# The last down-projection of a decoder step cut into five token spans instead of four, the last two of 128 tokens

## The chip, the cores and the metric

One core of one Trainium2 chip runs the whole step. The metric is the time of one execution in device microseconds (us); the median of three runs of the kernel before is 2002.76 us (2002.69 to 2004.21).

## What is computed

One step of a decoder layer for 1056 tokens: 1024 tokens of a new sequence and 32 tokens of 8 running ones (4 each), all with 1024 features. A SwiGLU feed-forward half, a mixer (recurrence and short convolution), a second SwiGLU half, and a last RMSNorm. Each sub-layer is modulated by a conditioning vector (shift, scale, gate). What matters here is the end of it:

```python
    hn = modulate(rmsnorm(x, g_ffn2), mod[:, 6], mod[:, 7])
    x = x + 0.5 * mod[:, 8][:, None, :] * swiglu(hn, w2_gate, w2_up, w2_down)
    ...
    y_prompt = rmsnorm(xp, final_gain)
    y_sample = rmsnorm(xs, final_gain)
```

## The kernel before, in words

Activations lie transposed: features on the 128 partitions, in 8 blocks of 128 features (KD = 8), tokens along the free dimension (N = 1056, of which T = 1024 are the prompt). A float32 product is made of three float32r matmuls: each operand is split into a high and a low part, and `accumulate` (L416) issues high x high, high x low and low x high for each block of the contraction, one bank of PSUM collecting all of them. Each of these matmuls loads its own 128x128 weights; the moving operand is as wide as the token span.

Most of the work before the end uses a Strassen form. The down-projection of the second half ends in two plain pieces of 512 contraction rows: `back` (L698) does the first with all three 352-token spans beside each other, and `last2` (L1423) does the second through `back_by_span` (L707), which is the end stage. Its outer loop runs over the spans of `END_SPANS` (L38), its inner one over the 8 output blocks o. For each (span, o):

- TensorE: 12 matmuls (4 blocks of contraction by 3 parts) into one bank (`accumulate`, L420). All 8 blocks' weights stay in SBUF, split into high and low, from the first span on.
- VectorE: `add_back` (L685) adds the gated bank onto x (L687); in the span that holds the 32 sample tokens two small operations more (L691, L693).
- ScalarE: the square of the new x (`square_add`, L546), and x times the final gain (L720). VectorE adds the squares into two accumulators (L550), and joins them at o = 6 (L552).

When a span is done, a generator (`norm_then`, L728, and `stats`, L556) is queued. It is advanced once per o of the next span (from o = 1). Per span it cuts the tokens into pieces of at most 128: a 256-token span has 2, a 272-token span 3 (128, 128 and 16), a 128-token span 1. It then
- sums the squares over the partitions with matmuls against ones ("nrm", L566): 4 TensorE instructions a piece, as two accumulators times two instructions of a float32 matmul;
- turns them into 1/rms with five small VectorE operations (L569, L571 to L574) and one ScalarE square root (L570);
- scales an identity by it ("dg", L580), one VectorE operation a piece;
- after a lag (2 steps for the first span, 3 for the others) spreads it over the partitions with matmuls ("rb", L587), 2 TensorE instructions a piece.
Then `final` (L1416) multiplies x by it on VectorE in three steps (4, 2 and 2 feature blocks, L1419) and sends each to HBM on SyncE's queue (L1420). In the last span no matmuls are left to hide this: `flush` (L410, called at L1427) runs it to the end.

The order in which the engines take these instructions is the framework's scheduling of the traced program; in this stage no order is written out by hand.

Of the kernel before, what the change touches and what calls it, by code (L numbers as in the profile page):

```python
# [34 lines left out]

FIRST_SPANS = ((0, 352), (352, 176), (HALF, 352), (HALF + 352, 176))
QUARTERS = ((0, Q), (HALF, Q), (Q, Q), (HALF + Q, Q))
END_SPANS = ((800, 256), (0, 272), (272, 272), (544, 256))  # L38

COL = {}  # L40
NPAR = 0
# [197 lines left out]
def decoder_step(ctx, tc, xin, par, ada0, ada1, ada2, wada, wf, wga, wdn, wdl, wmi, wgt, wmo,  # L239
# [467 lines left out]
    def back_by_span(kind, idx, buf, ms, after, spans=SPANS, gain=None):  # L707

        ids = [u for i in idx for u in ws.take(kind, i)]
        left = len(adas[1])  # L710
        for c, sp in enumerate(spans):
            accs = []
            for o in range(KD):
                b = bank(f"bk{o}_{sp[0]}")
                ahead = min(AHEAD, 7 - o) if c == 0 else 3 if sp == spans[-1] and o > 3 else 0
                accumulate([b], [sp], ws.unit(ids[o], ahead), rows(ms), True, True)
                add_back(buf, o, sp, b)
                square_add(accs, sp, o, join=gain is not None)
                if gain is not None:
                    act.activation(x[:, o, of(sp)], x[:, o, of(sp)], AF.Identity, scale=col(gain, o, o + 1))  # L720
                if o > 0:
                    advance()
                if sp == spans[-1] or left > KD and c > 0:
                    more_ada(-(-left // (KD * (1 + (left > KD)))))
            sums.append((("n", sp), norm_then(accs, sp, after, int(c > 0), 2 if c == 0 else 3)))
        assert not adas[1]
# [696 lines left out]
    def last2(kind, buf, ms):  # L1423
        back_by_span(kind, [(1, h) for h in range(4)], buf, ms, final, END_SPANS, "gf")

# [124 lines left out]
```

## Time and profile before

| | us |
|---|---|
| median of 3 runs | 2002.76 |
| the profiled execution | 2002.88 |
| its span in the trace | 2000.8 |
| TensorE busy | 1945.4 (97% of the span) |
| VectorE busy | 1288.1 (64%) |
| ScalarE busy | 757.8 (38%) |

The span is the time from the first to the last instruction in the trace; the profiled execution's own time is 2.1 us longer, which lies around it. "PE" is TensorE's matmuls, "PEld" its weight loads, "DVE" VectorE, "ACT" ScalarE, "SPq" the queue on which SyncE issues transfers. A line number such as L420 is the kernel's.

### The profile page before, as it was taken

The page shows a single profiled execution, that of the slowest core. Times are in us where ns is not written, and L with a number is a line of the kernel's source. Part 1 is how long each engine was busy: PE and PEld are TensorE (multiplying, and loading weights), DVE is VectorE, ACT ScalarE, POOL GpSimd, SP SyncE. Part 2 cuts the span into 40 slices and gives each one's busy share as a digit, 9 for nine tenths or more (in the row PEclk, how much of TensorE's full clock was granted, in tenths as well). Part 3 has the DMA queues.
Part 4 walks back from the last instruction along what each step waited for, and adds up shares of the span by engine and source line. Part 5 has one row for each costly group of instructions (what it writes and reads, how often), then busy time and mean ns, then how long its engine had stood idle before and what let it go on. Part 6 is the DMA issues. An engine that isn't in the chain of part 4 may idle for free.

```text
span 2000.8 us, 36465 instructions
## 1 busy us (share of the span) xinstructions
PE 1945.4 (97%) x15188; PEld 1913.1 (96%) x15188; DVE 1288.1 (64%) x2519; ACT 757.8 (38%) x1330; POOL 126.1 (6%) x223
## 2 busy tenths in 40 slices
PE   3899999999999999999999999999999999999997
PEld 3789999999999999999999999999999999999997
DVE  5564555565467875584887768666555645878656
ACT  3442233333342432344443447433333333433324
POOL 0000000100011000000000010001000000100000
PEclk9899999999999999999999999999999999999999
DMA  7245455531254532011111122532322222742302
GB/s 253 77 165 190 165 175 185 190 117 65 86 192 144 194 113 91 22 48 53 48 43 54 43 79 76 178 132 101 120 81 102 92 86 98 258 148 90 140 33 87
DMA packets 89764, 230.67 MB, mean 115 GB/s; under 512 B 7776, under 2 KB 41568, under 8 KB 89600
## 3 DMA queue, kind: packets, MB, share of 16 engines
q1 hardware_dynamic: 64592, 137.40, 20.5%
q0 software_dynamic: 25008, 90.96, 12.7%
q8 instruction: 119, 1.95, 0.4%
q14 instruction: 45, 0.37, 0.1%
HBM read 180.63 MB, written 47.69 MB: 114 GB/s over the span
## 4 chain that ended last, share of the span: by engine, by line
PE 95%; DVE 3%; DMA 1%; ACT 1%; issue 0%; SPq 0%; DVEq 0%; ACTq 0%
PE bk L420 14%; PE up_a L459 13%; PE ga_a L459 13%; PE dn_a L459 9%; PE up_c L459 6%; PE ga_c L459 6%; PE dn_c L459 5%; PE up_b L459 3%; PE ga_b L459 3%; PE v L420 2%; PE dn_b L459 2%; PE b L420 2%; PE c L420 2%; PE x L420 2%; PE n L420 2%; PE ada L503 2%
## 5 line engine op out<-in xcount | busy, mean ns | idle before, releaser
L220 DVE TENSOR_TENSOR hl<-raw,hl 128x512 fp32r<-128x512 f32 x286 | 194.9, 687 | 202.7 <-ACT hl L219 202.3
L219 ACT ACTIVATE hl<-raw 128x512 fp32r<-128x512 f32 x286 | 175.8, 626 | 249.8 <-PE bk L420 104.6
L219 ACT ACTIVATE hl<-S_ga 128x512 fp32r<-128x512 f32 x176 | 111.0, 631 | 279.4 <-DVE S_ga L172 59.3
L459 PE MATMUL dn_a<-f,hl 128*128 128x264 f32 x1536 | 192.0, 284 | 0.1
L420 PE MATMUL bk<-ml,hl 128*128 128x352 f32 (+2 forms) x1248 | 189.5, 312 | 1.4 <-DVE x L687 1.4
L459 PEld LDWEIGHTS dn_a<-f,hl 128*128 128x128 f32 x1536 | 189.3, 188 | 0.3 <-ACT f L820 0.3
L420 PEld LDWEIGHTS bk<-ml,hl 128*128 128x128 f32 x1248 | 186.6, 188 | 1.9 <-DVE x L687 1.9
L220 DVE TENSOR_TENSOR hl<-S_ga,hl 128x512 fp32r<-128x512 f32 x176 | 121.4, 690 | 76.2 <-ACT hl L219 75.3
L687 DVE SCALAR_TENSOR_TENSOR x<-bk,modT,x 128x352 f32<-128x352 f32 (+6 forms) x160 | 81.4, 534 | 101.1 <-PE bk L420 100.4
L459 PE MATMUL ga_a<-hnT,hl 128*128 128x264 f32 x792 | 103.2, 286 | 0.0
L459 PE MATMUL up_a<-hnT,hl 128*128 128x264 f32 x792 | 102.7, 285 | 0.0
L459 PE MATMUL up_a<-hmT,hl 128*128 128x264 f32 x792 | 102.1, 284 | 0.0
L459 PE MATMUL ga_a<-hmT,hl 128*128 128x264 f32 x792 | 102.1, 284 | 0.0
L459 PEld LDWEIGHTS ga_a<-hnT,hl 128*128 128x128 f32 x792 | 98.9, 188 | 3.3 <-issue 0.8
L459 PEld LDWEIGHTS up_a<-hnT,hl 128*128 128x128 f32 x792 | 98.8, 188 | 2.5 <-ACT u1st L473 0.4
L459 PEld LDWEIGHTS up_a<-hmT,hl 128*128 128x128 f32 x792 | 98.8, 188 | 0.4 <-ACT u1st L473 0.4
L459 PEld LDWEIGHTS ga_a<-hmT,hl 128*128 128x128 f32 x792 | 98.8, 188 | 0.4 <-ACT g1st L473 0.4
L459 PE MATMUL dn_c<-f,hl 128*128 128x264 f32 x768 | 96.4, 284 | 0.0
L459 PEld LDWEIGHTS dn_c<-f,hl 128*128 128x128 f32 x768 | 94.8, 188 | 0.0
L821 DVE TENSOR_TENSOR f<-f 128x1056 fp32r<-128x1056 f32 x56 | 67.9, 1254 | 25.1 <-ACT f L820 25.1
L219 ACT ACTIVATE hl<-S_dn 128x512 fp32r<-128x512 f32 x64 | 39.9, 628 | 114.3 <-PE dn_a L459 29.7
L820 ACT ACTIVATE f<-f 128x1056 fp32r<-128x1056 f32 x56 | 57.7, 1078 | 48.2 <-DMA f<-mf 48.0
(455 smaller groups left out, 3722.1 us busy)
## 6 DMA issues: line engine op xcount, KB each, us to landing
raw<-wga SPq DMA_DIRECT2D x88, 512.0 KB, 3.4
f<-mf POOLq DMA_DIRECT2D x28, 1056.0 KB, 6.6
raw<-wada SPq DMA_DIRECT2D x56, 512.0 KB, 5.2
raw<-wdn SPq DMA_DIRECT2D x32, 512.0 KB, 3.4
mf<-mt POOLq DMA_DIRECT2D x48, 264.0 KB, 3.3
raw<-wmi SPq DMA_DIRECT2D x20, 512.0 KB, 3.2
ml<-ml POOLq DMA_DIRECT2D x16, 528.0 KB, 4.7
raw<-wdl SPq DMA_DIRECT2D x16, 512.0 KB, 3.3
```

Source lines behind the costliest of these rows:

```text
L219: self.nc.scalar.activation(hl[:, 0], src, AF.Copy)
L220: self.nc.vector.tensor_sub(hl[:, 1], src, hl[:, 0].bitcast(F32))
L420: pe.matmul(b[:, :sp[1]], hl[:, wh, k], rhs(k, h, sp), start=first and k == ks[0] and i == 0, stop=last and k == ks[-1] and i == 2)
L459: pe.matmul(b[:, 512 - Q + q * Q:512 + q * Q], hl[:, wh, k], forms[X_FORMS[i]][:, k, h, q * Q:q * Q + Q], start=new and k == 0 and j == 0, ...
L503: pe.matmul(ada_bank[u][32 * q:32 * q + 32, :ADA_W[u]], cst[:, k], raw[:, q], start=k == 0, stop=k == KD - 1, skip_group_check=True)
L687: dve.scalar_tensor_tensor(x[:, o, lo:lo + n], b[:, :n], modT[:, buf, GATE, o, 0:1], x[:, o, lo:lo + n], op0=ALU.mult, op1=ALU.add)
L820: act.activation(form[:, k:k + 2, 0], raw[:, k:k + 2], AF.Copy)
L821: dve.tensor_sub(form[:, k:k + 2, 1], raw[:, k:k + 2], form[:, k:k + 2, 0].bitcast(F32))
```

## The change

One line. The sample tokens (1024 to 1055) stay in the span that is done first, which now starts at 784 and is 272 tokens wide; then come 256, 272, 128 and 128 tokens. The 1056 tokens, the functions and the loops are the same; the outer loop of the end stage has five turns instead of four.

```diff
-END_SPANS = ((800, 256), (0, 272), (272, 272), (544, 256))
+END_SPANS = ((784, 272), (0, 256), (256, 272), (528, 128), (656, 128))
```

## Rows read from the trace of the kernel before

**Rows 1.** The page, part 1: busy time, share of the span, instructions of each engine.

```profile
PE 1945.4 (97%) x15188; PEld 1913.1 (96%) x15188; DVE 1288.1 (64%) x2519; ACT 757.8 (38%) x1330; POOL 126.1 (6%) x223
```

**Rows 2.** TensorE's timeline of the end: start, us, instructions in count, idle time before.

```profile
1950.24 0.95 PE L566 MATMUL nrm<-ones,sq 128*128 128x1 f32 x8
1951.05 3.24 PE L420 MATMUL bk<-ml,hl 128*128 128x272 f32 x24
1955.17 0.68 PE L587 MATMUL rb<-dg,ones 128*128 128x128 f32 x4 [0.88 <-DVE dg L580]
1955.61 10.80 PE L420 MATMUL bk<-ml,hl 128*128 128x272 f32 x84
1966.24 1.39 PE L566 MATMUL nrm<-ones,sq 128*128 128x1 f32 x12
1967.50 4.74 PE L420 MATMUL bk<-ml,hl 128*128 128x272 f32 x36
1972.08 0.74 PE L587 MATMUL rb<-dg,ones 128*128 128x128 f32 x6
1972.66 7.48 PE L420 MATMUL bk<-ml,hl 128*128 128x272 f32 x60
...
1986.15 3.07 PE L420 MATMUL bk<-ml,hl 128*128 128x256 f32 x24
```

**Rows 3.** The chain that ended last, after the last down-projection matmul: start, us, what.

```profile
1990.13 1.07 PE nrm L566 x8
...
1992.87 1.06 PE rb L587 x4
...
1993.96 1.22 DVE x L1419
...
1995.78 0.60 DVE x L1419
```

**Rows 4.** TensorE's timeline in two stretches, each of one width only.

```profile
1899.85 36.01 PE L420 MATMUL bk<-ml,hl 128*128 128x352 f32 x222
...
1935.98 11.38 PE L420 MATMUL bk<-ml,hl 128*128 128x256 f32 x95
```

**Rows 5.** 89.9 to 115.7 us, 352 and 176 wide by turns: weight loads, busy us, mean ns.

```profile
L942 PEld LDWEIGHTS second<-hn,hl 128*128 128x128 f32 x191 | 26.0, 189 | 0.0
```

**Rows 6.** Weight loads of the norm sums in the last span: start, us, count.

```profile
1979.86 1.43 PEld L566 LDWEIGHTS nrm<-ones,sq 128*128 128x128 f32 x12
```

**Rows 7.** Groups by line and shape, 1890 us to the end: busy us, mean ns.

```profile
L546 ACT ACTIVATE sq<-x 128x272 f32<-128x272 f32 x16 | 6.9, 430 | 10.4 <-DVE x L687 10.4
...
L546 ACT ACTIVATE sq<-x 128x256 f32<-128x256 f32 x16 | 6.7, 417 | 10.5 <-DVE x L693 5.5 <-DVE x L687 5.1
...
L687 DVE SCALAR_TENSOR_TENSOR x<-bk,modT,x 128x256 f32<-128x256 f32 x8 | 3.9, 481 | 2.6 <-PE bk L420 2.6
L687 DVE SCALAR_TENSOR_TENSOR x<-bk,modT,x 128x224 f32<-128x224 f32 x8 | 3.6, 451 | 2.2 <-PE bk L420 2.0
...
L1419 DVE TENSOR_TENSOR x<-x,rb 128x512 f32<-128x512 f32 x4 | 2.6, 680 | 0.0
...
L1419 DVE TENSOR_TENSOR x<-x,rb 128x1024 f32<-128x1024 f32 x2 | 2.4, 1222 | 1.0 <-PE rb L587 1.0
```

**Rows 8.** SyncE's queue at the end, and sizes of the output transfers with us to landing.

```profile
1995.24 1.96 SPq L1420 DMA_DIRECT2D yout<-x  x3
...
yout<-x SPq DMA_DIRECT2D x2, 512.0 KB, 3.0
yout<-x SPq DMA_DIRECT2D x4, 256.0 KB, 3.4
```

**Rows 9.** TensorE's timeline around 95 us, single matmuls: 352 and 176 wide by turns.

```profile
95.27 0.43 PE L942 MATMUL second<-hn,hl 128*128 128x176 f32 x2
...
95.35 0.35 PE L942 MATMUL second<-hn,hl 128*128 128x352 f32 x1
...
95.54 0.43 PE L942 MATMUL second<-hn,hl 128*128 128x176 f32 x2
```

## The prediction

> **What bounds the kernel now.** I read the busy times first, then TensorE's timeline over the last 50 us, then the chain that ended last. TensorE is busy for 97% of the span [rows 1]. In the end stage it goes from one group of matmuls to the next almost without a hole: one wait of 0.88 us, at 1955.17, for the first span's "dg" [rows 2]. So what is added to TensorE's stream here lengthens the kernel, and what VectorE and ScalarE do beside it costs nothing while they keep up. The last down-projection matmul ends at 1986.15 + 3.07 = 1989.22 [rows 2]. From there to the end of the span (2000.8) are 11.6 us in which one step waits for the other: squares, "nrm", 1/rms, "dg", "rb", the scaling by VectorE, and the output transfer [rows 3]. The change trades these two: more in the stream, less in the tail.
>
> **Term 1, the matmuls.** Each (span, block) takes 12 matmuls whatever its width, so a span is 96 of them, and four spans become five: 384 become 480. By width, two spans of 272 and one of 256 stay (their order changes, and all move together in one direction); one of 256 goes, two of 128 come. The price of one by width is the distance from start to start, not its duration in the trace, since matmuls overlap:
> - 352 columns: the stretch lasts 36.01 us and its last matmul hangs some 0.17 over the next start, as 1955.61 + 10.80 against 1966.24 shows [rows 2]; (36.01 - 0.17)/222 = 161 ns [rows 4].
> - 272 columns: (1966.24 - 1955.61)/84 = 126.5 ns [rows 2].
> - 256 columns: (11.38 - 0.17)/95 = 118 ns [rows 4].
>
> No row shows a stream of 128-column float32r matmuls. Two things lie near. In the kernel's first pair 352 and 176 columns alternate, each with its own 128x128 weights: (26.0 - 0.19)/190 = 136 ns a matmul, 272 a pair [rows 5]; less the 161 of the wide one, 110 are left for 176 columns. A straight line through 352 and 256 columns would give 118 - 80 x 0.45 = 82. So below some width a matmul stops getting cheaper. And the matmuls of "nrm", whose moving operand is one column, still load 128x128 weights at (1.43 - 0.19)/11 = 113 ns each [rows 6]. I read both as the same floor: a new set of weights every 110 ns or so, whatever streams through. 128 columns lie between one and 176, so I take 110 ns. The bounds: not above 118 (256 columns), and not below the 80 ns treated as a rival.
> Price: 192 x 0.110 - 96 x 0.118 = 21.1 - 11.3 = **+9.8 us** (at 118 ns +11.3).
>
> **Term 2, the norm's matmuls in the stream.** A 272-token span has three pieces, a 256-token span two, a 128-token span one. In both kernels that makes 10 pieces, but before 2 + 3 + 3 = 8 lie in the stream and 2 in the tail; after 3 + 2 + 3 + 1 = 9 and 1. A "nrm" block of 8 instructions takes 1951.05 - 1950.24 = 0.81 us, one of 12 takes 1.26; so one of 4 should take 0.36. The blocks in the stream go from 0.81 + 1.26 + 1.26 to 1.26 + 0.81 + 1.26 + 0.36: +0.36. "rb" blocks of 4 and 6 take 0.44 and 0.58 [rows 2], one of 2 about 0.22: by the same count +0.23. Each block costs a little where the wide matmuls resume: 36 of them after a block take 4.74 - 0.17 = 4.57 us, against 36 x 0.1265 = 4.55 [rows 2]. I round the sum to **+0.7 us**.
>
> **Term 3, the one wait in the stream.** The first span's norm has the shortest cover, 24 matmuls of the second span. They now are of 256 columns and not 272: 24 x (126.5 - 118) = 0.2 us less cover, with one "dg" more to make. **+0.3 us** on top of the 0.88; bounds 0 and 1.
>
> **Term 4, the tail.** Per step, with half the tokens:
> - VectorE's add-back at 256 columns takes 481 ns, at 224 451 [rows 7]: about 0.95 ns a column, so 0.36 us at 128. ScalarE's square goes from 417 ns to about 0.31 by the slope from 272 columns. Before, "nrm" started 0.91 us after the last matmul's end, held by an accumulator add that VectorE did after the add-back, and ended at 1990.13 + 1.07 = 1991.20, 1.98 after it [rows 3]. VectorE was late there because the final scaling of a 272-token span lay in between (it takes over 2.6 us: 1222 + 2 x 680 ns is what a 256-token one costs [rows 7]); now it is that of a 128-token one, about half. I expect 0.04 + 0.36 + 0.03 + 0.31 + 0.04 until the last square is there, then two float32 instructions, 0.4: 1.2 us. That saves 0.8.
> - The chain of small operations to "rb" is the same: 1992.87 - 1991.20 = 1.67 [rows 3]. "rb" has two instructions instead of four: 1.06 becomes about 0.63. That saves 0.4.
> - The final scaling ends 1995.78 + 0.60 - 1993.96 = 2.42 us after its start [rows 3]. At half the width the first part takes 0.68 [rows 7], the others about 0.41. But SyncE issues three transfers in 1.96 us [rows 8], the last of them late only because its data were; at some 0.42 a piece, the last can go 0.84 after the first, 1.56 after the start. That saves 0.9.
> - The last transfer halves from 256 to 128 KB. 512 KB land in 3.0 us and 256 KB in 3.4 [rows 8], so size sets nothing here: 0.1 saved, bounds -0.5 and +0.5. The three transfers more (15 for 12) go through SyncE's queue, which carries nothing else then.
>
> Together **-2.25 us** (bounds -1.5 and -3.2).
>
> **Costed at nothing.** In a 128-token span TensorE needs 12 x 0.11 = 1.32 us a block. VectorE needs 0.36 + about 0.28 for the squares' sum, ScalarE 0.31 + about 0.41: covered, each with half of the time to spare. The samples' extra operations stay in the first span, which gets 16 columns wider.
>
> **Sum.** 9.8 + 0.7 + 0.3 - 2.25 = +8.55 us. Against the profiled execution's own 2002.88 us that is 2011.4; the median of the runs is 0.1 lower, which changes nothing.
>
> **The rivals.**
> *A: matmuls may start before their weights are all in (not slower).* In the first pair a 176-column matmul starts at 95.27, the next 352 at 95.35, the next 176 at 95.54 [rows 9]. The distances are 80 and 190 ns, so the 272 may also be shared out that way: 80 for the narrow one. If a stream of 128 columns ran at 80 ns, term 1 were 192 x 0.080 - 11.3 = +4.0 and the whole +2.8: 2005.7, no change that can be measured. Against it: no row shows a weight load every 80 ns in succession, and [rows 6] has 113 where nothing wide streams. It decides from about 86 ns downwards. Chance 8%.
> The Trainium skill, TensorE: Matmul & The Clock Gate, section Back-to-back issue gap, gives about 81 ns per matmul for sustained pairs of weight load and matmul at 128 columns; by that the sum would be rival A's. The same sentence gives about 131 ns at 512 columns, and the trace has 161 at 352 already [rows 4], so I lean on it little.
> *B: time follows the columns.* The line through 352 and 256 columns goes on to 118 - 128 x 0.45 = 60 ns. Term 1 is then +0.2 and the whole -1.0: 2001.9, again no measurable change. [Rows 5] speak against it: 60 + 0.45 x 48 = 82 for 176 columns, 243 a pair, not 272. Chance 3%.
> *C: VectorE falls behind.* In the first 128-token span VectorE also has the 272-token span's final scaling, over 2.6 us, beside 8 x 0.64 us of its own and some 1.5 us of 1/rms and "dg": 9.2 of 10.6 us. If "dg" is late there and in the next span, TensorE waits as it does in the tail, where the chain takes 1.67 us [rows 3]; the cover is 3 blocks, 3.96 us, so at most some 1.2 us each is lost: 2.4 more, 2013.8. It decides where add-backs and final scaling stand ahead of the small operations. Chance 8%.
>
> **How the numbers follow.** The forecast has 79%, A 8%, B 3%, C 8%; 2% is left for a gain that I don't see. 0.2%, about what a measurement of this kernel can tell from no change, is 4.0 us. So slower 87%, the same 11%, faster 2%. The forecast's own range is 2009.0 to 2013.2 (term 1 from 9.4 to 11.3, waits up to 1, tail from -3.2 to -1.5). I give 2008.0 to 2013.5: it leaves out A and B (11%), and the worse part of C.
>
> **What would show it.** Right: 480 down-projection matmuls in the stage, those of 128 columns 108 to 113 ns from start to start; one block of 4 "nrm" and of 2 "rb" instructions more in the stream; from the last down-projection matmul to the end of the span 9.1 to 9.6 us, not 11.6. Wrong: 128-column matmuls at 80 ns or less (A, B), or idle time of TensorE before "rb" in the last two spans (C).

## The result, and the profile after

The changed kernel takes 2027.28 us (median of 4 runs, 2026.55 to 2030.88) against 2002.99 us: 1.0121 times the time before, with a 95% interval from 1.0109 to 1.0133. It is slower, as forecast, but by 24 us and not by 8.5; that lies above the forecast's range of 2008.0 to 2013.5. The profiled execution took 2026.55 us, its span is 2024.6 us.

The page's lines for TensorE's matmuls and for its granted clock in 40 slices (tenths of full speed):

```profile
PE 1974.6 (98%) x15284; PEld 1942.6 (96%) x15284; DVE 1293.8 (64%) x2541; ACT 762.5 (38%) x1347; POOL 126.4 (6%) x223
...
PEclk9899999999999999999999999999999999999995
```

96 matmuls, each with its weight load, are what a fifth span adds to the count of [rows 1]. New is the last digit of the clock: the last slice ran at half speed. The next view puts numbers on it. A row gives a stretch and its length, the busy time (and instructions) of TensorE's matmuls, its weight loads, VectorE, ScalarE and GpSimd, then the granted clock, and last the share and rate of the DMA. The first two stretches lie within the first narrow span ("narrow" is 128 tokens wide); the third runs from there to the last span's norm; the fourth is the tail, 8.9 us, all of it at half clock too.

```profile
1975.00:1980.00 5.00, 5.00 (x47) 5.00 (x47) 2.23 (x6) 2.69 (x7) 0.00 (x0) 1.00 0.46 147
1980.30:1985.30 5.00, 5.00 (x26) 5.00 (x25) 2.31 (x11) 1.17 (x4) 0.00 (x0) 0.50 0.00 0
...
1979.89:2015.53 35.64, 35.64 (x171) 35.64 (x170) 13.70 (x44) 9.13 (x27) 0.00 (x0) 0.50 0.15 47
2015.73:2024.60 8.87, 1.71 (x6) 1.24 (x6) 2.79 (x10) 0.91 (x3) 0.00 (x0) 0.50 0.20 59
```

In 5 us TensorE starts about 47 matmuls at a granted clock of 1.00 (2.4 GHz) and about 25 at 0.50 (1.2 GHz). It is busy for all of both stretches: "busy" cannot show this. TensorE's timeline (start, us, instructions in count, idle time before), beginning with the last 352-token matmuls before the end stage:

```profile
1899.85 34.88 PE L420 MATMUL bk<-ml,hl 128*128 128x352 f32 x215
...
1954.75 0.81 PE L587 MATMUL rb<-dg,ones 128*128 128x128 f32 x6 [1.06 <-DVE dg L580]
...
1971.54 7.21 PE L420 MATMUL bk<-ml,hl 128*128 128x272 f32 x60
1978.59 1.45 PE L566 MATMUL nrm<-ones,sq 128*128 128x1 f32 x12
1979.89 7.68 PE L420 MATMUL bk<-ml,hl 128*128 128x128 f32 x36
1987.37 1.40 PE L587 MATMUL rb<-dg,ones 128*128 128x128 f32 x6
1988.61 13.04 PE L420 MATMUL bk<-ml,hl 128*128 128x128 f32 x60
2001.45 0.95 PE L566 MATMUL nrm<-ones,sq 128*128 128x1 f32 x4
2002.26 7.92 PE L420 MATMUL bk<-ml,hl 128*128 128x128 f32 x36
2009.98 0.74 PE L587 MATMUL rb<-dg,ones 128*128 128x128 f32 x2
2010.37 5.36 PE L420 MATMUL bk<-ml,hl 128*128 128x128 f32 x24
```

The line at 1971.54 holds the last 24 matmuls of 272 columns and the first 36 of 128: 7.05 us to the next start, less 24 x 0.1265 [rows 2], leaves 4.0 us, or 111 ns for each narrow one. That is the price the prediction took. After the norm's 12 instructions 36 narrow ones take 7.48 us, 208 ns each, and the next 60 take 12.84, 214 ns each: twice the price, to the end. All 192 take 4.0 + 7.5 + 12.8 + 7.7 + 5.2 = 37.2 us, where one span of 256 took 11.4.

Where the time went, from the two traces:
- the two narrow spans for the one of 256: 37.2 - 11.4 = +25.8 us, 16 more than forecast;
- the norm's "nrm" and "rb" blocks in the stream: +1.9 (the blocks at half clock also cost double, "rb" of 6 took 1.24 us at 1987.37 and 0.58 at 1972.08 before [rows 2]);
- the wait for the first "dg": 1.06 against 0.88, +0.2;
- the tail, 2024.6 - 2015.7 = 8.9 us against 11.6: -2.7.

That is +25.2. The spans differ by 23.8, because the end stage began 1.3 us earlier in this execution (1899.85 + 34.88 - 0.17 = 1934.6 against 1935.9 [rows 4], where the first of 96 matmuls lies 0.12 before the 95 shown). The change has no part in this; the last section says where the clock does.

The chain that ended last (start, us, what), from the last down-projection matmuls:

```profile
2013.81 1.93 PE bk L420 x9
...
2016.52 0.60 PE nrm L566 x2
...
2018.69 0.81 PE rb L587 x2
...
2019.53 0.69 DVE x L1419
...
2020.55 0.33 DVE x L1419
```

From 2015.74 the last "nrm" ends after 1.4 us (1.98 before), "rb" starts 1.57 later (1.67), takes 0.81 (1.06), and the final scaling takes 1.35 (2.42), against [rows 3]. The tail does shrink, as the narrower last span let one expect.

### The profile page after: what moved, and what is told of

It reads as the page before. It is cut to its first block, busy times and chain, and to the rows that moved or that the text cites. A ratio compares the mean times of both kernels' runs of the same rounds, so it can differ in the third digit from the quotient of the medians.

```text
span 2024.6 us, 36702 instructions
## 1 busy us (share of the span) xinstructions
PE 1974.6 (98%) x15284; PEld 1942.6 (96%) x15284; DVE 1293.8 (64%) x2541; ACT 762.5 (38%) x1347; POOL 126.4 (6%) x223
## 4 chain that ended last, share of the span: by engine, by line
PE 96%; DVE 3%; ACT 1%; DMA 0%; issue 0%; DVEq 0%; SPq 0%; ACTq 0%
PE bk L420 15%; PE up_a L459 13%; PE ga_a L459 13%; PE dn_a L459 9%; PE up_c L459 6%; PE ga_c L459 6%; PE dn_c L459 5%; PE ga_b L459 3%; PE up_b L459 3%; PE dn_b L459 2%; PE v L420 2%; PE b L420 2%; PE c L420 2%; PE x L420 2%; PE n L420 2%; PE ada L503 2%
## 5 line engine op out<-in xcount | busy, mean ns | idle before, releaser
L420 PE MATMUL bk<-ml,hl 128*128 128x352 f32 (+3 forms) x1344 | 215.6, 325 | 1.4 <-DVE x L687 1.4
L420 PEld LDWEIGHTS bk<-ml,hl 128*128 128x128 f32 x1344 | 212.6, 205 | 1.9 <-DVE x L687 1.9
L687 DVE SCALAR_TENSOR_TENSOR x<-bk,modT,x 128x352 f32<-128x352 f32 (+7 forms) x168 | 83.2, 519 | 117.2 <-PE bk L420 116.4
```

The source lines that it names most:

```text
L420: pe.matmul(b[:, :sp[1]], hl[:, wh, k], rhs(k, h, sp), start=first and k == ks[0] and i == 0, stop=last and k == ks[-1] and i == 2)
L687: dve.scalar_tensor_tensor(x[:, o, lo:lo + n], b[:, :n], modT[:, buf, GATE, o, 0:1], x[:, o, lo:lo + n], op0=ALU.mult, op1=ALU.add)
```

## The experiments

The forecast's own arithmetic needs a clock at full speed. The first question was whether the clock is the whole error, the second what brings it down, since the narrow matmuls began at full clock. The letters K, S, N and M stand for theories that the expectations below introduce.

**Same spans, wider streams.** In the two 128-token spans each matmul streams more columns than the span uses (256, with both spans' tokens, or 176). The edit, with `{width}` and `last_lo` in the place of the numbers that differ:

```diff
-                accumulate([b], [sp], ws.unit(ids[o], ahead), rows(ms), True, True)
-                add_back(buf, o, sp, b)
+                msp = sp if sp[1] != 128 else ({528: 528, 656: last_lo}[sp[0]], width)
+                accumulate([b], [msp], ws.unit(ids[o], ahead), rows(ms), True, True)
+                add_back(buf, o, sp, b[:, sp[0] - msp[0]:])
```

Here `last_lo` is 528 for 256 columns and 608 for 176. Expected with 256 columns:

> The changed kernel, but in its two last spans each matmul streams 256 columns (both spans' tokens) into the bank, and the rest of the span uses only its own 128. Spans, norms, transfers and tail stay as in the changed kernel. Theory K (the clock: a stream of 128-column matmuls runs at 110 ns until the granted clock falls to half, then at 213 ns, and the fall follows from the narrow stream): the clock stays at 1.0 to the tail, 256 columns take 118 ns, so the time is 2002.9 + 96 x 0.118 + 0.7 + 0.3 - 2.25 = about 2013 us. Rival S (the structure: a fifth span, its norm blocks and waits bring the clock down): the clock falls as in the changed kernel, 256 columns take 213 ns, about 2027 us.

Expected with 176 columns:

> The same with 176 streamed columns in the two last spans, 128 of them used. Theory K with the prediction's term 1 right at full clock: 110 ns a matmul and the clock at 1.0, about 2011.5 us. If the clock falls at 176 columns too, 213 ns and about 2027 us; the kernel before has 176 columns only by turns with 352, so this is open. If narrow matmuls are not held by the weight loads, 82 ns, about 2006 us.

Measured, each over 10 runs: 2012.69 us with 256 columns, 1.0043 times the kernel before (1.0030 to 1.0055), and 2012.38 with 176, 1.0036 times (1.0023 to 1.0049). Each matmul streams more columns, and the kernel takes 15 us less than the changed one. Stretches of both (256, then 176) from the first narrow span's start to the last matmul; the granted clock stands after the busy times:

```profile
1974.11:1999.50 25.39, 25.39 (x218) 25.26 (x216) 15.53 (x51) 12.01 (x35) 0.00 (x0) 1.00 0.28 90
```

```profile
1978.78:2003.20 24.42, 24.25 (x218) 24.09 (x216) 15.64 (x52) 11.88 (x35) 0.00 (x0) 1.00 0.29 95
```

The run with 176 columns also settles the price of a narrow matmul. One line of its timeline:

```profile
1984.06 4.24 PE L420 MATMUL bk<-ml,hl 128*128 128x176 f32 x36
```

That is (4.24 - 0.17)/36 = 113 ns. Rival S, that a fifth span by itself brings the clock down, is out: both kernels have the five spans and their norms. With the 111 ns that 128 columns took at full clock above, rivals A and B of the prediction are out too.

**A later norm.** The norm of the 272-token span, whose 12 "nrm" instructions lay in the first narrow span, is put off:

```diff
-            sums.append((("n", sp), norm_then(accs, sp, after, int(c > 0), 2 if c == 0 else 3)))
+            sums.append((("n", sp), norm_then(accs, sp, after, 6 if sp == (256, 272) else int(c > 0), 2 if c == 0 else 3)))
```

> The changed kernel with one norm moved: the sums of the 272-token span before the first 128-token span come after 6 or more blocks of that span instead of 3. Theory K in its plain form (the narrow stream alone brings the clock down): the clock falls as before some 4 us after the first 128-column matmul, with no norm block in between, and the time stays about 2027 us. Rival N (the block of 12 one-column matmuls after 24 narrow ones brings it down): 72 or more matmuls at 110 ns until the norm block, the clock falls only there, about 2022 us.

Measured: 2027.39 us, one run. By its time alone it would speak for theory K. The stretches say otherwise (all 96 matmuls of the first narrow span; the norm block and what follows up to the fall; the rest):

```profile
1983.34:1994.01 10.67, 10.67 (x99) 10.67 (x97) 5.51 (x17) 6.17 (x17) 0.00 (x0) 1.00 0.25 81
1994.01:1997.28 3.27, 3.27 (x32) 3.27 (x31) 1.93 (x11) 0.81 (x3) 0.00 (x0) 1.00 0.00 0
1997.30:2016.00 18.70, 18.70 (x90) 18.70 (x89) 7.53 (x23) 5.07 (x15) 0.00 (x0) 0.50 0.19 61
```

A whole narrow span, 10.67 us, ran at 1.00, 111 ns a matmul; the clock fell 2 us after the end of the norm block that now came behind it. From the first narrow matmul to the end of the last one it took 33.1 us, 8.1 less than the 41.1 of the changed kernel. In this execution, though, the first narrow span started 8.8 us later (1983.34 against 1974.6), which hides the gain in the sum. Theory N named the place of the fall rightly, and theory K came out at the measured time by accident.

**One narrow span only.**

```diff
-END_SPANS = ((784, 272), (0, 256), (256, 272), (528, 128), (656, 128))
+END_SPANS = ((784, 272), (0, 320), (320, 336), (656, 128))
```

> Four spans of 272, 320, 336 and 128 tokens: one narrow span, the last. Theory K: the first 30 to 40 of the 96 narrow matmuls at 110 ns, the rest at 213, tail partly at half clock: matmuls 41.0 + 16.7 against 47.0 us, +10.7; norms +0.5, wait -0.5, tail -1.9: about 2011.7 us. If the clock held in a single narrow span, all 96 at 110 ns: about 2005.3 us.

Measured: 2011.86 us, 1.0037 times (1.0023 to 1.0050). Its narrow span in two stretches:

```profile
1979.64:1987.00 7.36, 7.36 (x69) 7.36 (x67) 4.33 (x17) 3.11 (x10) 0.00 (x0) 1.00 0.37 127
1987.05:1997.15 10.10, 10.10 (x49) 10.10 (x49) 5.61 (x12) 2.85 (x8) 0.00 (x0) 0.50 0.23 79
```

The fall is there again, 2 us behind the norm block of 12, which ended at 1984.93. About 55 of the 96 narrow matmuls ran at full clock, more than the 30 to 40 expected. One narrow span is enough.

**No norm between the narrow matmuls.** Both norms that lay there wait until all matmuls are done:

```diff
-            sums.append((("n", sp), norm_then(accs, sp, after, int(c > 0), 2 if c == 0 else 3)))
+            sums.append((("n", sp), norm_then(accs, sp, after, 99 if sp[0] in (256, 528) and gain is not None else int(c > 0), 2 if c == 0 else 3)))
```

> The changed kernel with the norms of its last 272-token span and of its first 128-token span put off until all down-projection matmuls are done, so that the 192 narrow matmuls run with no norm matmul between them. Theory M (the narrow stream alone holds the clock; a block of one-column norm matmuls in it brings it down): the clock stays at 1.0, all 192 stand 110 ns apart, 21.2 us, and the tail grows by two norms: 2012 to 2016 us. Theory K (the narrow stream alone brings it down, only more slowly where no norm block lies in it): the clock falls within the 21 us, and most of the second span stands 213 ns apart, 2020 us or more.

Measured: 2017.7 us, one run, 1.7 above the range expected with the clock held. The narrow spans began 1.5 us later here than in the changed kernel, and from the last narrow matmul to the end of the span it took 18.2 us. The stretches: all 192 narrow matmuls; the norm block behind them; the tail.

```profile
1976.14:1997.53 21.39, 21.39 (x195) 21.39 (x193) 10.07 (x31) 11.86 (x33) 0.00 (x0) 1.00 0.13 41
1997.53:1998.46 0.93, 0.93 (x11) 0.93 (x10) 0.55 (x2) 0.31 (x1) 0.00 (x0) 1.00 0.00 0
1998.50:2010.00 11.50, 4.75 (x22) 4.49 (x22) 7.34 (x26) 0.90 (x4) 0.00 (x0) 0.50 0.39 123
```

The 192 matmuls took 21.39 us, 111 ns each, at full clock. The narrow stream alone did not bring it down in this execution; 0.9 us into the norm block behind it, the clock fell. Theory K is out for the 21 us that the two spans last.

**A shorter norm block.** VectorE adds the last block's square into the accumulator too, so a piece of the norm needs 2 TensorE instructions and not 4. The sums are the same but for the order of the additions.

```diff
-        if k in (0, 1, KD - 1):
+        if k in (0, 1) or k == KD - 1 and not join:
             accs.append(sq)
         else:
-            dve.tensor_add(accs[k % 2], accs[k % 2], sq)
+            dve.tensor_add(accs[k % len(accs)], accs[k % len(accs)], sq)
```

> The changed kernel with the last block's square added into the accumulator by VectorE as well, so that each piece's norm sum takes 2 TensorE instructions instead of 4: blocks of 6, 4, 6 and 2 in the stream instead of 12, 8, 12 and 4. If the length of the norm block is what brings the clock down (M): the clock holds, 18 instructions in place of the 32 of the kernel before save 1.5 us, and the time is 2002.9 + 8.6 - 1.9 = about 2009.6 us. If the block's length does not matter, the clock falls as in the changed kernel: 2025 us.

Measured over 10 runs: 2010.01 us, 1.0028 times the kernel before (1.0015 to 1.0041). The spans and matmuls are still 128 wide, and it takes 17 us less than the changed kernel. The stretch from the first narrow matmul to 0.65 us behind the last, and two lines of the timeline:

```profile
1971.62:1995.60 23.98, 23.33 (x210) 23.19 (x208) 16.51 (x54) 12.02 (x36) 0.00 (x0) 1.00 0.32 102
```

```profile
1975.58 0.78 PE L566 MATMUL nrm<-ones,sq 128*128 128x1 f32 x6
...
1980.91 6.90 PE L420 MATMUL bk<-ml,hl 128*128 128x128 f32 x60
```

The block of 6 leaves the clock at 1.00, and 60 narrow matmuls take 6.73 us, 112 ns each, where the changed kernel needed 12.84.

**A block of 8.** The second and third span change places, so that the norm in the first narrow span is of 256 tokens, 8 instructions:

```diff
-END_SPANS = ((784, 272), (0, 256), (256, 272), (528, 128), (656, 128))
+END_SPANS = ((784, 272), (256, 272), (0, 256), (528, 128), (656, 128))
```

> The changed kernel with its second and third span exchanged (272, 272, 256, 128, 128 tokens), so that the norm block in the first narrow span has 8 instructions instead of 12; the sums are made as in the changed kernel. Theory M says that the block between narrow matmuls decides, and it held with 6 and fell with 12; 8 lies between. If the clock holds, 2002.9 + 8.6 = about 2011 us; if it falls in the first narrow span, 2025 to 2027 us; if a rival theory is right by which joining the sums helped in another way than by the block's length, it falls here as with 12.

Measured: eight executions of it took 2010.73 and 2011.65 us (two, mean granted clock 0.992 and 0.991) and 2026.44 to 2032.76 (six, 0.981 to 0.984); beside it the kernel before took 2003.92. The profiled one is of the six:

```profile
1982.91:1989.30 6.39, 6.39 (x60) 6.39 (x59) 3.79 (x14) 3.42 (x10) 0.00 (x0) 1.00 0.47 153
1989.40:2021.70 32.30, 32.30 (x153) 32.30 (x153) 12.03 (x37) 8.63 (x25) 0.00 (x0) 0.50 0.15 49
```

The same program sometimes loses the clock and sometimes doesn't. The changed kernel was that long in all 4 executions; with joined sums none of 10 was (the longest took 2015.77). One execution of each kernel has a trace; of the others the clock is read from the time and the mean clock alone, and a loss in a few of the narrow matmuls would not stand out there. The run does not part the two readings well: as the block of 8 mostly loses the clock, that joining the sums helped in another way than by the block's length is not ruled out.

**Narrow spans early.** Wide spans follow the narrow ones:

```diff
-END_SPANS = ((784, 272), (0, 256), (256, 272), (528, 128), (656, 128))
+END_SPANS = ((784, 272), (528, 128), (656, 128), (0, 256), (256, 272))
```

> The changed kernel's five spans in another order: 272, 128, 128, 256, 272 tokens, so that wide matmuls follow the narrow ones. Theories M and K alike: the clock falls in the first narrow span after the norm block, about 30 to 40 matmuls at 110 ns and the other 150 to 160 at 213, 37 us for the two; then, if the wide stream gives the clock back within 3 to 10 us, 2 to 5 us more, and a tail as in the kernel before: 2032 to 2036 us. If the clock does not come back, the 192 wide matmuls stand about 220 ns apart and it is 2050 us.

Measured: 2030.63 us, one run. From the first narrow matmul; from the fall to the last narrow one; the first wide ones; the rest:

```profile
1948.50:1954.90 6.40, 6.40 (x60) 6.40 (x59) 3.40 (x15) 4.71 (x11) 0.00 (x0) 1.00 0.00 0
1954.95:1988.64 33.69, 33.69 (x161) 33.69 (x159) 12.42 (x38) 9.03 (x26) 0.00 (x0) 0.50 0.15 49
1988.64:1992.40 3.76, 3.76 (x19) 3.76 (x20) 0.83 (x2) 1.05 (x3) 0.00 (x0) 0.50 0.02 4
1992.50:2016.00 23.50, 23.48 (x194) 23.26 (x192) 15.78 (x43) 13.77 (x31) 0.00 (x0) 1.00 0.11 34
```

That is 1.4 us below the range expected. The clock comes back 3.8 us after 256-column matmuls begin. In the 33.7 us of narrow ones before them it did not. So here the loss lasted as long as the narrow matmuls did: after one block of 12 instructions all of them cost double.

**Fewer spans.** The opposite direction, on the kernel before, with the joined sums:

```diff
-END_SPANS = ((800, 256), (0, 272), (272, 272), (544, 256))
+END_SPANS = ((672, 384), (0, 416), (416, 256))
```

> The kernel before with three end spans of 384, 416 and 256 tokens, and the last square added by VectorE as in the run joined. No narrow matmuls, one norm block less in the stream, blocks of 6 and 8 instructions instead of 8, 12 and 12 (-1.9 us), rb blocks 6 and 8 instead of 4, 6 and 6 (-0.2), the 0.88 us wait covered by 24 matmuls of 190 ns (-0.9): about 2000 us if the final scaling of 416 tokens does not make VectorE late in the last span; 2001 us if it does.

Measured: 2003.87 us over 12 runs, 0.9999 times (0.9987 to 1.0010): nothing that can be told from no change, and not the gain of 2 to 3 us that was expected. The stream is shorter (49.5 us from the first matmul of the stage to the end of the last, against 53.4), but VectorE, busy with 416 tokens' final scaling, was late with the last sum, as the timeline and two lines of the chain that ended last show:

```profile
1991.42 0.61 PE L566 MATMUL nrm<-ones,sq 128*128 128x1 f32 x4 [3.06 <-DVE sq L550]
```

```profile
1985.50 1.88 DVE x L1419
...
1988.12 0.92 DVE x L1419
```

TensorE waits 3.06 us there, against 0.91 before the same block in the kernel before, from 1989.22 to 1990.13 [rows 2, 3].

## Why the prediction was wrong

The direction and the mechanism of the loss were right: the fifth span's weight loads cost more than the shorter tail gives. The size failed in **term 1**, at the step that multiplied all 192 narrow matmuls by 0.110 us. The price was right while the granted clock was 1.00: 111 ns in the first 36, 111 in norms_at_end, 112 in joined. From 1980.2 on the clock was 0.50, and the same matmul took 213. The floor that I had read from [rows 5] and [rows 6] is one at full clock, and I never asked whether the clock would stay; none of the three rivals held this either. Had it stayed, the forecast of +8.55 us would have held: with 176 columns, the same floor and the clock at 1.00, the kernel took 2012.38, +8.5 on the 2003.91 of the kernel before beside it. With joined sums it took 2010.01, for which the same arithmetic gave 2009.6; that is +5.6 on the 2004.41 beside it, against +6.7.

What brings the clock down in the end stage is shown by taking its parts one by one. Narrow matmuls alone did not do it in the 21 us of norms_at_end, a single execution. Norm blocks of 12 between wider matmuls did not, with 256 or 176 columns or in the kernel before, whose two blocks of 12 lie in this stretch:

```profile
1955.60:1989.20 33.60, 33.60 (x279) 33.41 (x277) 23.68 (x59) 18.50 (x42) 0.00 (x0) 1.00 0.22 72
```

The two together did, in the changed kernel (in all four runs by their times), in one128, late_norm, early_narrow and norms_at_end, each time 0.9 to 3.8 us after a norm block of 12 had begun. Half the block, with one more add on VectorE, did not in the execution traced. Why the two together do it, no run here measures. It is not idleness: TensorE was busy for 5.00 of 5.00 us on either side of the fall.

The Trainium skill, TensorE: Matmul & The Clock Gate, section HAM oscillation — how this bites in real kernels, gives idle waits of TensorE between its groups of matmuls as the cause of such falls. Here the trace differs: no idle time of TensorE stands in the timeline between 1971.54 and the fall.

The kernel before held a warning, if a weaker one, that I did not look for. Two stretches earlier in its run, at a block of norm matmuls near 870 us, behind the first feed-forward half (busy time and clock as above):

```profile
870.00:870.50 0.50, 0.50 (x4) 0.50 (x4) 0.50 (x3) 0.14 (x1) 0.00 (x0) 0.55 0.51 205
...
872.00:874.00 2.00, 2.00 (x13) 2.00 (x11) 0.00 (x0) 0.00 (x0) 0.00 (x0) 0.63 0.00 0
```

```profile
869.72 0.68 PE L566 MATMUL nrm<-ones,sq 128*128 128x1 f32 x4 [1.59 <-DVE ab L691]
```

The clock fell within the norm block that the timeline shows at 869.72, and came back between 873 and 874; TensorE was busy throughout. But this block has only 4 instructions, wide matmuls follow it, and TensorE had idled for 1.59 us in front of it, which it does not before the fall in the end stage. The trace does not tell which of these mattered, so it shows that the clock can fall, and not that a norm block does it. The prediction says nothing of the clock, in this stretch or in any other.

The other points:
- Term 2 (+0.7): measured +1.9, as the blocks too ran at half clock.
- Term 3 (+0.3): the wait grew by 0.2.
- Term 4 (-2.25): -2.7, inside its bounds, although "nrm" and "rb" took 0.60 and 0.81 at half clock; the final scaling and the last transfer gave more than I took.
- Rivals A and B: out; no stream of 128 or 176 columns ran below 110 ns. Rival C: out; VectorE's "dg" was never waited for in the narrow spans, where TensorE was slow enough to cover anything; with joined sums, at full clock, it was not waited for there either.

## What to carry to other kernels

Before narrowing a matmul's moving side, price it twice: at the floor set by its weight load, and at twice that, in case the granted clock falls. Read the clock by stretches, since busy time shows neither. One-column matmuls (sums against ones) in a stream that already waits on weight loads are a risk of their own: here the form with half of them took 17 us less, and once the clock had fallen every narrow matmul behind it cost double. And the end of a kernel is shortened only if what is added to the stream is less: 192 loads for 96 cost 10 us even at full clock, for a tail 2 to 3 us shorter.

## What was not expected

- A norm block of 8 lost the clock in six executions of eight: the same program took 2011 to 2012 or 2026 to 2033 us. A single time near such an edge says little, and late_norm, norms_at_end and early_narrow are single executions.
- The weight-load floor follows the clock: 111 ns at 1.00, 213 at 0.50, for matmuls of 128 columns.
- Some of the spread of all these runs (the kernel before took 1999.6 to 2010.6 us over 23 executions beside the joined sums) comes from the clock at another place, the stretch behind 870 us, which the change does not touch. In late_norm it ran at half clock for longer than in the kernel before, in the changed kernel at full clock (late_norm first):

```profile
872.00:880.00 8.00, 8.00 (x32) 8.00 (x32) 4.47 (x15) 1.76 (x4) 0.00 (x0) 0.50 0.00 0
...
872.00:880.00 8.00, 8.00 (x54) 8.00 (x54) 7.49 (x22) 2.85 (x6) 0.00 (x0) 1.00 0.00 0
```

  The same norm block, with the same wait of 1.59 us, lies in front of it in all three. From that block to the second group of "b" matmuls behind it the changed kernel took 8.5 us, the kernel before 10.0 and late_norm 13.2. The changed kernel gained 1.6 us on the kernel before here, more than the 1.3 us by which its end stage began earlier; late_norm lost 4.7 us on the changed kernel, of the 8.8 by which its narrow spans began later. Of the 11 traces 4 show a fall there, in code that is the same. Whether this explains all of the spread was not tried.
